# A hybrid attention block on one core: the scheduler's machine model is exchanged

## The chip, the cores and the metric

The kernel runs on one NeuronCore of a Trainium2 chip. The metric is the device time of one execution in microseconds (us). The core has a matrix engine (PE, TensorE), three engines for elementwise work (DVE, the vector engine; ACT, the scalar engine; POOL, GpSimd) and SP (SyncE), which here only issues DMAs. Each engine works through its own list of instructions in order. Between engines, semaphores hold an instruction back until what it reads is written and what it overwrites has been read.

## What is computed

One layer of a streaming encoder on 512 rows of width 1024, all in float32. Three sub-layers, each with an RMS norm before and after it, are added to the residual:

```python
h = rms_norm(x, g_mix_pre)
q_f, k_f, v_f, f_logit, q_c, k_c, v_c = jnp.split(h @ w_in, splits, axis=-1)
o_f = fox_attention(q_f, k_f, v_f, log_sigmoid(f_logit + b_fgate))   # 8 heads of 64, causal
o_c = chunked_rel_attention(q_c, k_c, v_c, rel_bias)                 # 8 heads of 64, banded
mix = jnp.concatenate([rms_norm(o_f, g_fox_out), rms_norm(o_c, g_chunk_out)], -1) @ w_out
x = x + rms_norm(mix, g_mix_post)
ca = memory_cross_attention(rms_norm(x, g_mem_pre), rms_norm(mem, g_mem_kv), w_mem_q, w_mem_kv, w_mem_o)
x = x + rms_norm(ca, g_mem_post)                                     # 4 heads of 256, 256 memory rows
x = x + rms_norm(swiglu(rms_norm(x, g_ffn_pre), w_gate_up, w_down), g_ffn_post)
```

## The kernel before

Every large float32 product is made of three matmuls: each operand is split into a high part `hi` and a rest `lo`, and `mm3` (lines 142 to 146) adds hi·hi, lo·hi and hi·lo into one PSUM bank. Weights come by DMA into three `raw` buffers (line 121); ACT makes `hi` by a cast (line 125) and DVE `lo` by a subtraction (line 126), into two buffers each. A *unit* is one such piece of weights, numbered in the order of use.

The work in the order of the program, with the time it takes place in the profiled execution before:

- 0 to 52 us: x is loaded and normalised, V of the first groups, q and k of the first group.
- 59 to 239 us: sixteen attention heads. `head` (line 524) takes four blocks of 128 rows. For each block PE makes the scores (lines 533 and 534), DVE adds the bias and takes the maximum (line 537), ACT makes the exponential and its sum (line 547), DVE the reciprocal (line 548) and the product with it (line 549), PE the transposes (line 552), ACT the high part of the transposed probabilities, `pth` (line 554), DVE the rest, `ptl` (line 555). After four blocks PE multiplies with V (line 561), ACT and DVE combine the two halves (lines 569 and 570). `pair_out` (line 572) does the split of each pair's output (lines 573 and 574). The probabilities `p` have three buffers.
- Between the heads stand dense matmuls that don't depend on them: q, k and V of later groups (`group_proj`, line 404, and `proj_blocks`, line 383, whose bank is emptied on DVE at line 391 and split on ACT and DVE at lines 423, 424, 439, 440 and 443) and the half of the output projection that needs only the first eight heads (lines 649 to 659, banks `ps_a387` to `ps_a394`). Heads 9 to 16 take their bias by a DMA (`chunk_bias`, line 516) into one of four buffers.
- `mem_norm` (line 591) normalises the memory (line 596) and splits it into `mT` (lines 599 and 600), at the end of the heads.
- 239 to 283 us: keys and values of the memory, from `mT` (the first bank is `ps_a402`), and the rest of the output projection. 295 to 400: cross-attention, with transposes at line 809. 400 to 465: its output projection and the start of the feed-forward part, with transposes at line 170.
- 465 to 644 us: a stage whose order on PE, DVE and ACT is written out by hand (line 1227). 645 to 760: the down projection, then the end.

PSUM has eight banks, in four kinds: three `a` (dense products), two `s` (scores), two `t` (transposes), one `o` (the products with V).

Outside the written-out stage the order on each engine isn't that of the code. A scheduler of the language plays the program through with a model of the machine: at each step it takes, for an engine that the model has free, the instruction that is ready in the model's time, and among several the one of least priority number. The number is the place in the code, shifted by `later(n)` (line 96). Those that matter here are `later(-20)` for the projections of a group (line 609), `urge[n]` of −205, 150, 0 and −120 for the heads of the four groups (line 602), +100 more for the products with V (line 556), 135 for `mem_norm` (line 636) and −5 for the half of the output projection (line 649). What the model says an instruction takes, and what it waits for, therefore decides what is put in front of what, while on the chip the order is then fixed.

## Time and profile before

| | |
|---|---|
| median of 2 runs | 769.27 us (769.16 to 769.38) |
| the profiled execution, its own time | 769.24 us |
| its span in the trace | 767.5 us |
| PE busy | 752.7 us, 98% of the span |
| DVE busy | 595.7 us, 78% |
| ACT busy | 442.9 us, 58% |
| POOL busy | 63.6 us, 8% |
| TensorE clock granted, mean | 0.997 |
| DMA | 80.05 MB, 104 GB/s |

How to read it: busy time counts the time in which an engine had at least one instruction under way. Matmuls are pipelined, so that neighbours overlap and the busy time of one of them is longer than the distance to the next. In the rows, `L533 MATMUL ps_s<-T,Q` is an instruction of line 533 that writes the tile `ps_s` and reads `T` and `Q`; a number behind a name in the order rows below is the buffer or the tile's serial number.

### The profile page before, as it was taken

How to read it: one execution, taken by the hardware profiler on the slowest of the kernel's cores; microseconds unless marked ns; L12 is line 12 of the kernel's file. 1: busy time of each engine (PE TensorE's matmuls, PEld its weight loads, DVE VectorE, ACT ScalarE, POOL GpSimd, SP SyncE). 2: the span in 40 equal slices, each digit the busy share in tenths (PEclk: the TensorE clock that was granted, in tenths of full speed). 3: DMA queues.
4: the chain of work that ended last, by engine and by line, in shares of the span. 5: the costliest groups of instructions: out<-in, count | busy, mean ns of one | idle time of the engine just before them, and what ended most of it. 6: DMA issues, size and time to landing. Idle time of an engine off the chain costs nothing.

```text
span 767.5 us, 12862 instructions
## 1 busy us (share of the span) xinstructions
PE 752.7 (98%) x4988; PEld 674.4 (88%) x4988; DVE 595.7 (78%) x1083; ACT 442.9 (58%) x811; POOL 63.6 (8%) x105
## 2 busy tenths in 40 slices
PE   9999999999999999999999999999999999999996
PEld 9977888887778988877778899999999999898985
DVE  8667889789886688555653897999999999987746
ACT  7558889667875457444563635555555557543411
POOL 1001132100321201000001200000000000000001
PEclk9999999999999999999999999999999999999998
DMA  7522123422323735421341132333333323233312
GB/s 268 145 64 76 29 56 95 126 83 60 109 80 83 265 120 186 118 76 59 108 147 48 56 102 65 110 111 110 111 111 110 111 84 110 83 115 107 108 58 109
DMA packets 60748, 80.05 MB, mean 104 GB/s; under 512 B 2704, under 2 KB 43664, under 8 KB 60688
## 3 DMA queue, kind: packets, MB, share of 16 engines
q1 hardware_dynamic: 59264, 74.49, 30.9%
q0 software_dynamic: 1280, 4.72, 1.8%
q8 instruction: 39, 0.64, 0.4%
q14 instruction: 21, 0.17, 0.1%
q10 hardware_dynamic: 144, 0.02, 0.0%
HBM read 77.13 MB, written 2.10 MB: 103 GB/s over the span
## 4 chain that ended last, share of the span: by engine, by line
PE 87%; ACT 6%; DVE 4%; issue 2%; POOL 1%; DMA 1%; DVEq 0%; POOLq 0%; ACTq 0%
PE ps_a L144 13%; PE ps_a L146 13%; PE ps_a L143 13%; PE ps_t L1130 3%; PE ps_t L1127 3%; PE ps_s L1128 3%; PE ps_t L1128 3%; PE ps_s L1127 3%; PE ps_s L1130 3%; PE ps_s L143 2%; PE ps_s L146 2%; PE ps_s L144 2%; PE ps_t L552 2%; PE ps_o L561 2%; PE ps_s L533 1%
## 5 line engine op out<-in xcount | busy, mean ns | idle before, releaser
L126 DVE TENSOR_TENSOR lo<-raw,hi 128x1024 fp32r<-128x1024 f32 x56 | 68.2, 1223 | 20.6 <-ACT hi L125 20.4
L146 PE MATMUL ps_a<-hTh,lo 128*128 128x512 f32 x192 | 76.7, 399 | 0.0
L144 PE MATMUL ps_a<-hTl,hi 128*128 128x512 f32 x192 | 75.9, 395 | 0.0
L143 PE MATMUL ps_a<-hTh,hi 128*128 128x512 f32 x192 | 75.9, 395 | 0.0
L125 ACT CAST hi<-raw 128x1024 fp32r<-128x1024 f32 x56 | 57.8, 1047 | 25.5 <-PE ps_a L144 21.2
L923 DVE TENSOR_TENSOR ring_lo<-sums,ring_hi 128x1024 fp32r<-128x1024 f32 (+1 forms) x39 | 46.7, 1196 | 12.9 <-ACT ring_hi L922 8.5
L922 ACT CAST ring_hi<-sums 128x1024 fp32r<-128x1024 f32 (+1 forms) x39 | 40.1, 1029 | 17.2 <-PE ps_s L1128 15.6
L922 ACT CAST ring_hi<-fraw 128x1024 fp32r<-128x1024 f32 (+1 forms) x26 | 26.7, 1033 | 33.5 <-DVE fraw L1009 13.9
L923 DVE TENSOR_TENSOR ring_lo<-fraw,ring_hi 128x1024 fp32r<-128x1024 f32 (+1 forms) x26 | 31.0, 1201 | 14.2 <-ACT ring_hi L922 14.0
L144 PEld LDWEIGHTS ps_a<-hTl,hi 128*128 128x128 f32 x192 | 36.1, 188 | 6.4
L146 PEld LDWEIGHTS ps_a<-hTh,lo 128*128 128x128 f32 x192 | 36.1, 188 | 6.4
L143 PEld LDWEIGHTS ps_a<-hTh,hi 128*128 128x128 f32 x192 | 36.2, 188 | 5.6
L547 ACT ACTIVATE p<-p,nm 128x128 f32<-128x128 f32 (+1 forms) x64 | 36.1, 565 | 8.1 <-DVE nm L537 7.2
L554 ACT CAST pth<-ps_t 128x128 fp32r<-128x128 f32 (+1 forms) x64 | 27.0, 424 | 14.5 <-PE ps_t L552 13.7
L555 DVE TENSOR_TENSOR ptl<-ps_t,pth 128x128 fp32r<-128x128 f32 (+1 forms) x64 | 30.7, 487 | 5.0 <-ACT pth L554 3.7
L552 PE MATMUL ps_t<-ident,p 128*128 128x128 f32 x160 | 28.2, 275 | 1.1 <-DVE p L549 0.8
L549 DVE TENSOR_SCALAR p<-p,rc 128x128 f32<-128x128 f32 (+1 forms) x64 | 26.8, 418 | 0.1
L552 PEld LDWEIGHTS ps_t<-ident,p 128*128 128x128 f32 x160 | 19.3, 140 | 7.3 <-issue 2.4
L143 PE MATMUL ps_a<-hi,oh 128*128 128x512 f32 x64 | 25.5, 399 | 0.0
L1130 PE MATMUL ps_a<-b,ring_lo 128*128 128x256 f32 (+1 forms) x93 | 25.5, 276 | 0.0
L1127 PE MATMUL ps_a<-b,ring_hi 128*128 128x256 f32 x92 | 25.5, 277 | 0.0
L1128 PE MATMUL ps_a<-b,ring_hi 128*128 128x256 f32 x92 | 25.4, 276 | 0.0
(546 smaller groups left out, 2760.9 us busy)
## 6 DMA issues: line engine op xcount, KB each, us to landing
raw<-in_dram SPq DMA_DIRECT2D x64, 512.0 KB, 3.9
fraw<-in_dram SPq DMA_DIRECT2D x26, 512.0 KB, 3.5
place<-in_dram SPq DMA_DIRECT2D x21, 512.0 KB, 4.3
more_room<-in_dram SPq DMA_DIRECT2D x15, 512.0 KB, 4.3
cb<-in_dram SPq DMA_DIRECT2D x8, 256.0 KB, 2.7
xo<-in_dram POOLq DMA_DIRECT2D x4, 512.0 KB, 7.6
out_dram<-yd SPq DMA_DIRECT2D x8, 256.0 KB, 2.0
rawv<-in_dram SPq DMA_DIRECT2D x3, 520.0 KB, 6.3
```

Of the source, the lines that this page charges most:

```text
L125: act.copy(hi[:, j : j + n, :], raw)
L126: dve.tensor_tensor(out=lo[:, j : j + n, :], in0=raw, in1=f32(hi[:, j : j + n, :]), op=ALU.subtract)
L143: pe.matmul(dst, sh, mh, start=first, stop=False)
L144: pe.matmul(dst, sh, ml, start=False, stop=False)
L146: pe.matmul(dst[:, to], sl, mh[:, to], start=False, stop=last)
L547: act.activation(p[:, :n], p[:, :n], AF.Exp, bias=nm, scale=-1.0, accum_out=sm)
L552: pe.transpose(tp[:, k * P : (k + 1) * P], p[:, k * P : (k + 1) * P], ident)
L922: act.copy(h2, v)
L923: dve.tensor_tensor(out=l2, in0=v, in1=f32(h2), op=ALU.subtract)
L1127: pe.matmul(dst, w[0][:, k, :], b[:, 0, k, :], start=first and k == 0, stop=False, skip_group_check=more)
L1128: pe.matmul(dst, w[0][:, k, :], b[:, 1, k, :], start=False, stop=False, skip_group_check=more)
L1130: pe.matmul(dst[:, to], w[1][:, k, :], b[:, 0, k, to], start=False, stop=last and k == 3, skip_group_check=more,)
```

## The change

It hands the context that schedules the program one more argument. The instructions are the same 7012 in both programs; only the order on the engines differs.

```diff
@@ -1517,7 +1517,7 @@
     args.append(nc.dram_tensor("out_0_dram", (SEQ, D), _mybir.dt.float32, kind="ExternalOutput").ap())
-    with _tile.TileContext(nc) as tc:
+    with _tile.TileContext(nc, schedule_with_timeline_sim=True) as tc:
         hybrid_block_kernel(tc, *args)
```

The order is the same from 465 us of before through the written-out stage and in the last 60 us. It differs on PE, DVE and ACT in the attention heads, in the cross-attention, in the start of the feed-forward part and in the first 55 us of the down projection. Three places show it; the first is on PE, at the score matmul of head 11, block 2 (`ps_s262_2078`; `ps_a296` and `ps_a297` are projections of the last group, `ps_a394` is the last bank of the half output projection). Before:

```order
L552 MATMUL ps_t245_2004<-ident_69,p10_2_1996 128x128 x3
L146 MATMUL ps_a296_2337<-hTh_82,lo8_2212 128x512
L143 MATMUL ps_a297_2369<-hTh_82,hi8_2211 128x512
L144 MATMUL ps_a297_2369<-hTl_83,hi8_2211 128x512
L533 MATMUL ps_s262_2078<-T101_1859,Q101_1783 128x384
L534 MATMUL ps_s262_2078<-L2_420,Q101_1783 128x384
L552 MATMUL ps_t250_2021<-ident_69,p10_3_2013 128x128 x4
L146 MATMUL ps_a297_2369<-hTh_82,lo8_2212 128x512
L143 MATMUL ps_a297_2369<-hTh_82,hi8_2211 128x512
```

After:

```order
L144 MATMUL ps_a394_2964<-lo11_2847,oh_623 128x512
L146 MATMUL ps_a394_2964<-hi11_2846,ol_624 128x512
L552 MATMUL ps_t245_2004<-ident_69,p10_2_1996 128x128 x3
L533 MATMUL ps_s262_2078<-T101_1859,Q101_1783 128x384
L534 MATMUL ps_s262_2078<-L2_420,Q101_1783 128x384
L552 MATMUL ps_t250_2021<-ident_69,p10_3_2013 128x128 x4
L533 MATMUL ps_s267_2095<-T101_1859,Q101_1783 128x512
L534 MATMUL ps_s267_2095<-L2_420,Q101_1783 128x512
L561 MATMUL ps_o251_2028<-pth1_410,V10_1597 128x512
L552 MATMUL ps_t256_2058<-ident_69,p11_0_2050 128x128
L561 MATMUL ps_o251_2028<-ptl1_411,V10_1597 128x512
```

All 166 dense matmuls from `ps_a297` to `ps_a394` that stood behind this score matmul now stand ahead of it, and behind it no dense matmul follows until `ps_a402`.

The second place is on DVE, in the heads 12 and 13 (`p12`, `p13`: probabilities of these heads; `qk`: a projection on its way out of PSUM; `lo10`: the rest of weight unit 10). Before:

```order
L548 RECIPROCAL rc286_2165<-sm285_2164 128x1
L555 TENSOR_TENSOR ptl1_411<-ps_t282_2154,pth1_410 128x2x128
L549 TENSOR_SCALAR p12_2_2162<-p12_2_2162,rc286_2165 128x384
L537 ISA p12_3_2179,nm289_2180<-ps_s288_2176,cb3_2125 128x512
L537 ISA nm289_2180 128x1
L570 TENSOR_TENSOR o11_2043<-ps_o272_2113,ot11_2122 64x512
L391 TENSOR_TENSOR qk_2394<-ps_a297_2369,rrow_67 128x512
L126 TENSOR_TENSOR lo10_2402<-raw10_0_2403,hi10_2401 128x1024
L555 TENSOR_TENSOR ptl1_411<-ps_t287_2170,pth1_410 128x3x128
L548 RECIPROCAL rc291_2182<-sm290_2181 128x1
L424 SCALAR_TENSOR_TENSOR Q111_2396<-qk_2394,Q111_2396 64x512
L549 TENSOR_SCALAR p12_3_2179<-p12_3_2179,rc291_2182 128x512
```

After:

```order
L537 ISA p12_3_2179,nm289_2180<-ps_s288_2176,cb3_2125 128x512
L537 ISA nm289_2180 128x1
L549 TENSOR_SCALAR p12_2_2162<-p12_2_2162,rc286_2165 128x384
L548 RECIPROCAL rc291_2182<-sm290_2181 128x1
L537 ISA p13_0_2497,nm301_2498<-ps_s300_2494,cb4_2491 128x128
L537 ISA nm301_2498 128x1
L549 TENSOR_SCALAR p12_3_2179<-p12_3_2179,rc291_2182 128x512
L570 TENSOR_TENSOR o11_2043<-ps_o272_2113,ot11_2122 64x512
L555 TENSOR_TENSOR ptl1_411<-ps_t282_2154,pth1_410 128x2x128
L555 TENSOR_TENSOR ptl1_411<-ps_t287_2170,pth1_410 128x3x128
L548 RECIPROCAL rc303_2500<-sm302_2499 128x1
L537 ISA p13_1_2512,nm306_2513<-ps_s305_2509,cb4_2491 128x256
```

The rows of the projections and weights (lines 126, 391, 424) have left this place for one further ahead; reductions, reciprocals, products and subtractions of neighbouring blocks follow one another.

The third place is on PE, in the cross-attention, at the first transposes of line 809 (`ps_t444`; `ps_a452` and `ps_a466` are projections to the queries of later heads, `ps_s` scores). Before:

```order
L144 MATMUL ps_a452_3809<-hTl2_3420,hi23_3656 128x512
L146 MATMUL ps_a452_3809<-hTh2_2998,lo23_3657 128x512
L143 MATMUL ps_a452_3809<-hTh2_2998,hi23_3656 128x512
L809 MATMUL ps_t444_3742<-ident_69,xp0_3720 128x128 x2
L144 MATMUL ps_a452_3809<-hTl2_3420,hi23_3656 128x512
L809 MATMUL ps_t444_3742<-ident_69,xp0_3720 128x128 x2
L146 MATMUL ps_a452_3809<-hTh2_2998,lo23_3657 128x512
L143 MATMUL ps_a452_3809<-hTh2_2998,hi23_3656 128x512
```

After:

```order
L146 MATMUL ps_a466_3952<-hTh2_2998,lo24_3800 128x512
L143 MATMUL ps_s454_3864<-kT_2997,qq_3421 128x256
L144 MATMUL ps_s454_3864<-kT_2997,qq_3421 128x256
L146 MATMUL ps_s454_3864<-kT_2997,qq_3421 128x256
L143 MATMUL ps_a466_3952<-hTh2_2998,hi24_3799 128x512
L144 MATMUL ps_a466_3952<-hTl2_3420,hi24_3799 128x512
L809 MATMUL ps_t444_3742<-ident_69,xp0_3720 128x128 x4
L146 MATMUL ps_a466_3952<-hTh2_2998,lo24_3800 128x512
L143 MATMUL ps_a466_3952<-hTh2_2998,hi24_3799 128x512
```

17 dense matmuls of the next block (`ps_a466`) and more of `ps_a453` stand between the scores and their transposes, and the four transposes stand together.

On SP the bias loads of heads 9 to 16 stand some places later among the loads of weights, among them those of heads 9 to 12 ahead of one weight load of the output projection; POOL's order is nearly unchanged.

## The prediction

> **What bounds the kernel now.** I read the page's head and its slices first, then the share of the chain by engine, then the waits of PE, then windows of the stretch that the change rearranges.
>
> ```profile
> PE 752.7 (98%) x4988; PEld 674.4 (88%) x4988; DVE 595.7 (78%) x1083; ACT 442.9 (58%) x811; POOL 63.6 (8%) x105
> ...
> PE   9999999999999999999999999999999999999996
> ...
> DVE  8667889789886688555653897999999999987746
> ...
> PEclk9999999999999999999999999999999999999998
> ...
> PE 87%; ACT 6%; DVE 4%; issue 2%; POOL 1%; DMA 1%; DVEq 0%; POOLq 0%; ACTq 0%
> ```
>
> PE is busy in 98% of the span and holds 87% of the chain: the kernel is bound by the number of matmuls, and almost nothing can be won. The waits of PE say how little: the longest is 1.1 us, at the start of the program (the first row), and those of the cross-attention and the start of the feed-forward part (lines 809 and 170) are the others here; columns: total us, times, longest.
>
> ```profile
> PE ps_t L241 <- DVE ones L80: 1.1, 1, 1.1
> ...
> PE ps_t L809 <- DVE xp L804: 0.7, 2, 0.5
> PE ps_t L170 <- DVE b L183: 0.4, 1, 0.4
> PE ps_t L170 <- DVE y L161: 0.2, 1, 0.2
> PE ps_t L170 <- DVE f L181: 0.2, 1, 0.2
> ```
>
> The bound is a mean over the span, though. In the attention, up to 239 us, softmax work on DVE and ACT and transposes on PE run in a chain, and dense matmuls of later projections fill the gaps. The windows show how close the second engine is there (columns: stretch, its length, busy time and instructions of PE, PEld, DVE, ACT, POOL, then clock, DMA share, GB/s).
>
> ```profile
> 173.10:239.10 66.00, 63.66 (x331) 50.60 (x329) 57.23 (x151) 51.40 (x109) 12.63 (x12) 1.00 0.24 73
> 62.40:173.10 110.70, 108.77 (x654) 93.40 (x654) 93.66 (x261) 88.41 (x208) 21.03 (x42) 1.00 0.25 72
> 404.47:420.79 16.32, 16.32 (x73) 13.52 (x72) 5.76 (x9) 4.99 (x9) 2.54 (x3) 1.00 0.11 32
> 640.00:660.00 20.00, 20.00 (x120) 17.65 (x119) 20.00 (x39) 12.97 (x21) 0.57 (x1) 1.00 0.38 132
> ```
>
> DVE has 57.23 of 66.0 us of work in the last six heads and 93.66 of 110.7 before them. Take the dense matmuls out of the first stretch and DVE, not PE, sets its length.
>
> **The dense matmuls that move.** The last place where both orders can be laid on one another is the first score matmul of head 11, block 2 (the first order pair above). Everything that stood ahead of it before stands ahead of it after, and 166 matmuls of 512 columns more: 70 of the q and k projections of the last group (buffers 297, 298, 299) and 96 of the half of the output projection that needs only the first eight heads (387 to 394). The rows of that moment before:
>
> ```profile
> 170.59 0.33 PE L533 MATMUL ps_s<-T,Q 128*128 128x384 f32 x1
> ...
> 173.15 0.54 DVE L537 CUSTOM_DVE_ANT_0 p<-ps_s,cb 128x384 f32<-128x384 f32 x1
> ```
>
> One dense matmul costs its slot, not its busy time, since neighbours overlap in the pipeline: the window at 404.47 holds nothing but 72 of them, with 72 weight loads, in 16.32 us, so 0.2267 us each. 166 × 0.2267 = 37.6 us, and the score matmul goes from 170.59 to about 208.2. [...]
>
> These 37.6 us aren't work added. They leave the stretch from the reduction of head 11, block 2, at 173.15, to the split of the memory at line 600, after which PE goes on with the memory's keys in both orders:
>
> ```profile
> 234.01 0.79 DVE mm L596 x2
> 234.82 1.92 ACT mT L599
> 236.76 2.30 DVE mT L600
> 239.11 0.38 PE ps_a L144
> ```
>
> PE's remainder in this stretch is at most 66.0 − 37.6 = 28.4 us. If the stretch could shrink to that, the move would cost nothing. It can't, because of DVE.
>
> **What DVE keeps in the bare stretch.** With the fillers go the DVE instructions that prepare or empty them. Busy time in the stretch, by line, in this order: 126 (split of weights), 391 (empty a projection), 424 and 440 (split q and k):
>
> ```profile
> 173.10:239.10 66.00, 7.55 (x6) 1.00 0.24 73
> ...
> 173.10:239.10 66.00, 2.04 (x3) 1.00 0.24 73
> ...
> 173.10:239.10 66.00, 2.75 (x4) 1.00 0.24 73
> ...
> 173.10:239.10 66.00, 2.73 (x4) 1.00 0.24 73
> ```
>
> Together 15.07 us, now (second order pair) under dense PE work further ahead: there DVE gets 93.66 + 15.07 = 108.7 us for 110.7 + 37.6 = 148.3 us of PE, which hides it. 57.23 − 15.07 = 42.2 us stay. Two subtractions of line 555 (three and four blocks wide) now stand behind line 600 and no longer delay it, −1.1 us by the mean of the group below (487 ns each, wider than the mean). So 41.1.
>
> ```profile
> L547 ACT ACTIVATE p<-p,nm 128x128 f32<-128x128 f32 (+1 forms) x64 | 36.1, 565 | 8.1 <-DVE nm L537 7.2
> ...
> L555 DVE TENSOR_TENSOR ptl<-ps_t,pth 128x128 fp32r<-128x128 f32 (+1 forms) x64 | 30.7, 487 | 5.0 <-ACT pth L554 3.7
> ...
> L549 DVE TENSOR_SCALAR p<-p,rc 128x128 f32<-128x128 f32 (+1 forms) x64 | 26.8, 418 | 0.1
> ```
>
> Is 41.1 us attainable on an engine that waits now and then? Two ends. Packed: neighbours on DVE overlap a little. The 128-column reduction before starts at 169.91, lasts 0.29, and its neighbour starts 0.22 later. If two thirds of the 134 instructions left save 0.07 each, 6.3 us go, and 34.8 are the lower end. Loose: if DVE stays as busy as before, 57.23 of 66.0, the 41.1 become 47.4. Between them lie the round trips from the reduction over the exponential (565 ns and its accumulator's read) to the reciprocal. The new order (second order pair) puts the multiply, subtract or reduction of a neighbouring block in between, so that I estimate 1 us a head over packed work: 34.8 + 5.4 heads × 1 = 40.2. I take 41.1, the busy time itself.
>
> ```profile
> 169.57 0.19 ACT L547 ACTIVATION_READ_ACCUMULATOR p<-p,nm 128x1 f32 x1
> ...
> 169.91 0.29 DVE L537 CUSTOM_DVE_ANT_0 p<-ps_s,cb 128x128 f32<-128x128 f32 x1
> 170.13 0.08 DVE L537 DVE_READ_ACCUMULATOR2_ANT nm<- 128x1 f32 x1
> ```
>
> The net of the move: +37.6 − (66.0 − 41.1) = +12.7 us. ACT can't bind: from its 51.40 us at least the casts of weights, q and k leave as well.
>
> **Weights that come late.** The projections run closer behind one another, and hi and lo have two buffers each, so a weight unit is split into the pair that the matmuls two units earlier have just read. For four units only 1.7 to 3.1 us of PE work (counted in the new order, at the slots of before) stand between the last reader and the first use; one cast and one split take
>
> ```profile
> L126 DVE TENSOR_TENSOR lo<-raw,hi 128x1024 fp32r<-128x1024 f32 x56 | 68.2, 1223 | 20.6 <-ACT hi L125 20.4
> ...
> L125 ACT CAST hi<-raw 128x1024 fp32r<-128x1024 f32 x56 | 57.8, 1047 | 25.5 <-PE ps_a L144 21.2
> ```
>
> 1.05 + 1.22 = 2.27 us. At 2.27 against 1.7 to 3.1, I take 0.25 us each, +1.0; ends 0 and +4 (a cast that finds ACT busy with an exponential, four times).
>
> **Cross-attention and start of the feed-forward part.** There the new order puts more dense matmuls ahead of the transposes that waited (third order pair). If the four waits above vanish, −1.5 us; ends 0 and −3, since each switch between transposes and dense matmuls has its own cost and there are fewer. I take −1.5.
>
> **The down projection.** The windows show DVE full, 20.00 of 20.00 us, at 640 to 660. One split moves behind two others there. The same work in another order under a full DVE: I take 0, ends −1 and +1.5.
>
> **POOL and SP.** The bias loads of the chunk heads stand some places later among SP's weight loads, and one weight load of the output projection stands behind four of them. The bias buffers they wait for are those of heads that end tens of us earlier: 0. POOL's order is nearly the same: 0. In the written-out stage and from 700 us on the order is the old one: 0.
>
> **Sum** against the profiled run, 769.24 us (span 767.5 and 1.7 around it; the median of the runs is 769.27): +12.7 + 1.0 − 1.5 + 0 = +12.2, so 781.4 us, 1.6% more. About 2%, 753.9 and 784.7 us, is what a measurement of this kernel can tell from no change.
>
> **Rivals.**
> First, DVE packs better than I think, and is over before it matters: 34.8 us give +6.4, with −1.5 and no late weights 774.1; fewer switches on PE could bring 771.5. For it: DVE showed 20.00 of 20.00 us busy at 640, so it can pack when fed. Against it: there its work is independent, here each multiply waits for an exponential. Even a stretch of 28.4 us would give only 767.7: faster by 2% can't be had by moving matmuls on an engine that is busy 98%.
> Second, on the slower side, the bare heads pack no better than the filled ones: three buffers of probabilities, two banks for scores and two for transposes hold the blocks in step, and PE's own queue, in order, makes each wait longer. At 47.4 us the move costs +19.0 and the total is 787.7. It decides from 44.3 us in the stretch (line 600 ending after 256) upward; late weights at their +4 end have the same effect from 41.3.
> Third, the clock. PE would be busy for 28.4 of 41 us. The trace of before shows what a nearly idle PE gets (0.27 of 7 us busy, clock 0.70), and what it keeps with gaps under 1.1 us (1.00):
>
> ```profile
> 760.00:767.00 7.00, 0.27 (x3) 0.07 (x1) 3.08 (x8) 1.02 (x4) 0.54 (x1) 0.70 0.39 150
> ```
>
> If the clock halved through the stretch, its 28.4 us would become up to 56.8, 15.7 more than DVE's 41.1, and the total 797. The gaps that I find between PE's instructions in the new order are about 1 us, so that it should keep 1.00. [...]
>
> **Chances.** The forecast (775 to 785) 0.52; the first rival (below 775) 0.18; the second (785 to 792) 0.25; the clock 0.03; faster by over 2% 0.02. The range of 8 in 10 runs from the first rival's 771.5 to 789, beyond the second's 787.7. Faster 0.02, within 2% 0.70, slower 0.28.
>
> **What would show it.** Right: the score matmul of head 11, block 2, starts near 209 (208 to 213); from the following reduction to the end of line 600 it takes 39 to 44 us, with DVE over 90% busy and PE 65 to 75%, clock 1.00; line 600 ends near 253; the lead of before stays about the same from there to the end, and shrinks by 1 to 2 us between 290 and 465. Wrong: heads after 209 with DVE under 88% busy (second rival), a clock below 0.95 there (third), or stalls over 1 us on line 143 at weight units before 209.

## The result: 812.7 us, 5.6% slower, and the profile after

The changed kernel takes 812.7 us (median of 2 runs, 811.81 and 813.60) against 769.27 before: ratio 1.056, 95% interval 1.0543 to 1.0577. The prediction was 781.4, its range ended at 789.0. The profiled execution took 813.60 us, its span is 811.6, 44.1 us longer than before.

From the page of the kernel after, the rows that answer those of before: busy time by engine, the busy slices of PE and DVE and the granted clock, and the chain by engine.

```profile
PE 771.5 (95%) x4988; PEld 690.1 (85%) x4988; DVE 596.6 (74%) x1083; ACT 444.5 (55%) x811; POOL 61.0 (8%) x105
...
PE   9999999989977799989998999999999999999996
...
DVE  8666679664788568735564379999999899988745
...
PEclk9999999999989799999999999999999999999999
...
PE 83%; DVE 7%; ACT 6%; issue 3%; DMA 0%; POOL 0%; DVEq 0%; POOLq 0%; ACTq 0%
```

The reader is to see three things. PE, at 90% or more in every slice but the last before, falls to between 70 and 80% in the twelfth to fourteenth slice (223 to 284 us). DVE is less busy than before in seven of the eight slices ahead of them. And the clock, 1.00 before up to the tail, drops there too (0.86 from 224.74 to 272.56 us). The waits of PE, whose longest was 1.1 us, now begin with these (total us, times, longest):

```profile
PE ps_s L533 <- DVE nm L537: 6.6, 11, 1.4
PE ps_t L552 <- DVE ptl L555: 4.2, 4, 2.0
PE ps_o L561 <- ACT pth L554: 2.5, 2, 1.8
PE ps_t L552 <- DVE rc L548: 2.2, 2, 1.9
PE ps_a L143 <- ACT hTh L179: 2.0, 1, 2.0
PE ps_a L143 <- ACT oT L825: 2.0, 3, 0.9
PE ps_a L143 <- DVE V L351: 1.6, 1, 1.6
```

The timeline of the kernel after gives the three moments on which the sum of the prediction rested:

```profile
219.54 0.44 PE L533 MATMUL ps_s<-T,Q 128*128 128x384 f32 x1
...
224.74 0.53 DVE L537 CUSTOM_DVE_ANT_0 p<-ps_s,cb 128x384 f32<-128x384 f32 x1
...
270.27 2.29 DVE L600 TENSOR_TENSOR mT<-mm,mT 128x2048 fp32r<-128x2048 f32 x1 [1.18 <-ACT mT L599]
```

Beside the starts of the same instructions before, and later ones taken from the timelines in the same way:

| moment | before | after | later by | forecast |
|---|---|---|---|---|
| score matmul of head 11, block 2 | 170.59 | 219.54 | 49.0 | 38.6 |
| its reduction on DVE | 173.15 | 224.74 | 51.6 | 38.6 |
| end of line 600 | 239.06 | 272.56 | 33.5 | 13.7 |
| rest of the output projection (`ps_a406`) | 261.69 | 298.90 | 37.2 | 13.7 |
| last bank of the projection after the cross-attention, first half (`ps_a497`) | 399.03 | 443.28 | 44.3 | 12.2 |
| written-out stage (`ps_t538`) | 465.17 | 508.75 | 43.6 | 12.2 |
| end of the span | 767.5 | 811.6 | 44.1 | 12.2 |

So every part of the attention cost more than forecast: the front by 10.4 us, the step to the reduction by 2.6, the bare stretch by 6.8, the memory's keys by 3.7. The cross-attention turned from −1.5 to about +7.

### The profile page after: what moved, and what is told of

The parts are those of the page before. It is cut to its first block, busy times and chain, and to the rows that moved or that the text cites. A ratio compares the mean times of both kernels' runs of the same rounds, so it can differ in the third digit from the quotient of the medians.

```text
span 811.6 us, 12892 instructions
## 1 busy us (share of the span) xinstructions
PE 771.5 (95%) x4988; PEld 690.1 (85%) x4988; DVE 596.6 (74%) x1083; ACT 444.5 (55%) x811; POOL 61.0 (8%) x105
## 4 chain that ended last, share of the span: by engine, by line
PE 83%; DVE 7%; ACT 6%; issue 3%; DMA 0%; POOL 0%; DVEq 0%; POOLq 0%; ACTq 0%
PE ps_a L143 14%; PE ps_a L144 14%; PE ps_a L146 14%; PE ps_t L1130 3%; PE ps_t L1127 3%; PE ps_s L1130 3%; PE ps_s L1127 3%; PE ps_t L1128 3%; PE ps_s L1128 3%; PE ps_s L143 2%; PE ps_s L144 2%; PE ps_s L146 2%; PE ps_o L561 1%; PE ps_a L1130 1%; PE ps_a L1128 1%
## 5 line engine op out<-in xcount | busy, mean ns | idle before, releaser
L146 PEld LDWEIGHTS ps_a<-hTh,lo 128*128 128x128 f32 x192 | 36.9, 192 | 9.7 <-DVE lo L126 2.5
L144 PEld LDWEIGHTS ps_a<-hTl,hi 128*128 128x128 f32 x192 | 36.9, 192 | 7.9 <-DVE hTl L183 0.9
L533 PE MATMUL ps_s<-T,Q 128*128 128x256 f32 (+1 forms) x64 | 24.0, 378 | 7.3 <-DVE nm L537 6.6
L1127 PE MATMUL ps_a<-b,ring_hi 128*128 128x256 f32 x92 | 25.5, 277 | 0.0
L144 PE MATMUL ps_a<-lo,oh 128*128 128x512 f32 x64 | 25.3, 395 | 0.2 <-DVE lo L126 0.2
```

Source lines behind the costliest of these rows:

```text
L144: pe.matmul(dst, sh, ml, start=False, stop=False)
L146: pe.matmul(dst[:, to], sl, mh[:, to], start=False, stop=last)
L1127: pe.matmul(dst, w[0][:, k, :], b[:, 0, k, :], start=first and k == 0, stop=False, skip_group_check=more)
```

## The experiments

Most of these kernels hold an order given from outside. They have the instructions of the kernel and this addition, which ties each instruction of an engine behind the one named ahead of it, for the issue only; `ORDER` is a table of names by engine.

```diff
         hybrid_block_kernel(tc, *args)
+        _in_order(tc, nc, _mybir, _lists(ORDER))
+
+def _in_order(tc, nc, mybir, lists):
+    at = {i.name: i for i in nc.cur_bb.bb.instructions}
+    issue_only = mybir.DependencyInfo(mybir.DependencyClass.NoSync, mybir.DependencyReason.DATA)
+    for row in lists:
+        for one, two in zip(row, row[1:]):
+            tc.add_manual_dep(at[two], one, issue_only, reason="order")
```

### Where the loss is made: two halves put together

The first kernel takes the lists of before up to the instructions that start by 239 us, and those of after behind them; the second the other way round.

> All engines keep the order of before up to the start of the memory's keys (239 us of before), and the order of after from there on. Theory: the loss has two parts of their own, about 37 us made in the attention and about 7 us made in the cross-attention and behind it by the order there; this run keeps only the second, so 774 to 780 us. Rival: the later part loses only because the attention hands it late weights and a cold clock; then 768 to 771 us.

> The order of after up to the start of the memory's keys, and the order of before from there on. Theory: 803 to 808 us, the attention's part alone, line 600 ending about 33 us later than before. Rival: 810 to 814 us, as after, since the later loss would follow from the attention.

Measured: 776.02 us (ratio 1.0083, 1.0054 to 1.0113) and 806.19 us (1.0475, 1.0437 to 1.0514). Both lie in the theory's span. 6.75 and 36.9 us add up to 43.7, and the whole loss is 43.4: the attention and the part behind it lose independently. The sum holds to some 2 us only, by which single runs of these kernels differ (805.19 and 807.20 for the second).

### The cross-attention: one place

> The order of before on all engines up to 320 us of before (the normalisation ahead of the cross-attention and its transposes included), the order of after from there on. Theory: of the 6.75 us that the later part cost alone, most (2.2 + 0.7 us of waits and about 1.7 us of half clock) come from one place, where two splits of a weight unit stand on ACT and DVE ahead of the normalised rows that PE waits for, and that place is now as before: 770.5 to 773 us. Rival: the loss sits in the output projection of the cross-attention (waits of 0.5 to 1.1 us six times): 774 to 777 us.

Measured: 771.78 us (1.0034, 1.0023 to 1.0045). About 4 of the 6.75 us are made between 239 and 320 us of before. The timeline of the kernel after shows where: ACT does two casts of weights (line 125) and DVE two splits (line 126) ahead of the short rows of lines 179 and 183, and PE stands for 2.05 us.

```profile
345.12 1.99 ACT L125 CAST hi<-raw 128x1024 fp32r<-128x1024 f32 x2
347.01 0.84 ACT L179 ACTIVATE hTh<-ps_t,gn 128x256 fp32r<-128x256 f32 x2
...
346.20 2.36 DVE L126 TENSOR_TENSOR lo<-raw,hi 128x1024 fp32r<-128x1024 f32 x2 [0.25 <-ACT hi L125]
...
347.54 0.97 PE L143 MATMUL ps_a<-hTh,hi 128*128 128x512 f32 x3 [2.05 <-ACT hTh L179]
```

The next kernel changes only this place of the kernel after; on ACT (on DVE lines 126 and 183 in the same way):

```diff
-L125 CAST hi_3656<-raw_0_3658 128x1024
-L125 CAST hi_3656<-raw_4_3662 128x1024
 L179 ACTIVATE hTh_2998<-ps_t_3570,gn 128x256
 L179 ACTIVATE hTh_2998<-ps_t_3579,gn 128x256
+L125 CAST hi_3656<-raw_0_3658 128x1024
 L179 ACTIVATE hTh_2998<-ps_t_3570,gn 128x256
 L179 ACTIVATE hTh_2998<-ps_t_3579,gn 128x256
+L125 CAST hi_3656<-raw_4_3662 128x1024
```

> The kernel after with one place changed, at 345 us: on ACT two, on DVE two of the rows that make the normalised input of the cross-attention's queries stand ahead of the casts and splits of weight unit 23 instead of behind them. Theory (PE waits 2.2 + 0.7 + 0.3 us for rows that stand behind 2.4 us of splits, and the low use that follows halves the clock for 3.4 us): the waits shrink to about 1 us, no half clock near 349, 808.5 to 810 us. Rival (the third dense matmul there needs unit 23 itself, so that the wait only moves to it): 811.5 to 813.5 us.

Measured: 809.82 us (807.29 to 810.71; 1.0516, 1.05 to 1.0532), 2.9 us below the median of after. The waits of PE between 330 and 360 us are now

```profile
PE ps_a L143 <- ACT hi L125: 0.6, 1, 0.6
PE ps_a L143 <- ACT hTh L179: 0.2, 1, 0.2
```

against 2.0 + 0.5 in after, and the half clock at 349 us is gone. In the profiled executions 0.7 us of the difference are there by `ps_a406` (298.16 instead of 298.90), ahead of the changed place, and 4.1 at the first transposes of line 809 (375.80 instead of 379.88): the order of the rows at this place costs about 3 us.

### The clock: more work, less time

The windows of the kernel after, cut in steps of 3.41 us from the edges of its half-clock stretches (the shortest ahead of the tail last 3.41 us; columns as in the prediction), in pairs: a window in which PE does little, and the next one.

```profile
168.20:171.61 3.41, 1.50 (x10) 0.84 (x8) 3.32 (x8) 2.22 (x7) 0.29 (x2) 1.00 0.32 90
171.61:175.03 3.42, 3.24 (x8) 2.57 (x9) 2.43 (x6) 2.74 (x5) 0.14 (x1) 0.50 0.02 5
181.85:185.27 3.42, 1.72 (x10) 1.29 (x11) 3.36 (x6) 1.89 (x4) 0.00 (x0) 1.00 0.58 169
185.27:188.68 3.41, 3.41 (x18) 3.41 (x18) 0.01 (x1) 0.00 (x0) 2.31 (x2) 0.50 0.43 138
...
345.69:349.11 3.42, 1.07 (x4) 0.59 (x4) 3.17 (x5) 2.29 (x5) 0.00 (x0) 1.00 0.21 70
349.11:352.52 3.41, 3.41 (x8) 2.64 (x9) 1.11 (x3) 0.74 (x2) 0.00 (x0) 0.50 0.90 258
```

In each pair the clock is 0.50 in the window that follows the one of low use (1.50, 1.72 and 1.07 us of PE work), though PE is busy for 3.24 to 3.41 us of it. In the second and third pair it is full of dense matmuls, which take nearly twice their time: those of 256 columns start 0.21 us apart instead of 0.11, those of 512 columns 0.43 instead of 0.23.

What the first two pairs cost is told by the second kernel of the two halves (the attention of after). Up to the memory's keys its order is that of after on every engine, and the waits of PE at these places are as long (1.2 us for line 555, 1.6 for line 351), but in its profile no window of the front is halved. From 165 to 195 us, after and then this kernel:

```profile
165.00:195.00 30.00, 25.87 (x134) 21.50 (x133) 16.10 (x29) 13.92 (x25) 4.03 (x6) 0.89 0.23 73
```

```profile
165.00:195.00 30.00, 25.85 (x147) 21.34 (x146) 18.22 (x38) 15.56 (x29) 5.64 (x8) 1.00 0.29 96
```

In the same 30 us it does 13 matmuls more. From 164 to 193 us it gains 3.1 us on after, half of it in each of the two windows, and its score matmul of head 11, block 2, starts at 217.01 instead of 219.54. Two more kernels leave the front of after as it is, the one with the place at 345 us and the one with less DVE work (below). Their profiles have one of the two half windows, and the score matmul starts at 218.76 and 218.62.

From 222.8 to 277.4 us the clock of after is halved for 20.5 us in all (6.83 + 3.41 + 10.24). To see what this costs, PE gets work that nobody needs (shown in part; a second table names the instructions ahead of which it stands):

```diff
+        tc.extra = extra = []
         with later(-115):
             for c in range(4):
                 hi, lo = unit()
                 acc = bank("a")
+                if c == 0:
+                    for _ in range(55):
+                        extra.append(pe.matmul(acc, oh[:, 0, :P], oh[:, 0, :], start=True, stop=True))
```

> The kernel after in its own order on every engine, with 55 matmuls of 512 columns more on PE (12.5 us at 0.2267 us each), whose products nobody reads (they go to the bank of the memory's first keys before it is begun). They stand ahead of 16 instructions for which PE waits in the last heads, each group shorter than that wait. Theory (PE is so little used there that the granted clock halves, and the half clock costs time): the clock stays at 1.00 from 219 to 280 us, and the kernel is 2 to 6 us faster than after, 807 to 811 us, in spite of 12.5 us more work on PE. Rival (the half clock costs nothing, since PE waits there anyway): same as after or slower, 812 to 820 us.

Measured: 810.32 us (808.72 to 813.59; 1.0535, 1.0506 to 1.0565), 2.4 us below after, though single runs overlap with it. The windows of this kernel, for the bare stretch and for 260 to 280, and below them those of after:

```profile
224.74:272.56 47.82, 40.66 (x209) 28.80 (x210) 40.79 (x131) 32.12 (x82) 11.96 (x12) 1.00 0.16 49
260.00:280.00 20.00, 16.29 (x106) 13.56 (x107) 12.53 (x32) 8.86 (x17) 2.58 (x4) 1.00 0.01 1
```

```profile
224.74:272.56 47.82, 34.12 (x162) 25.30 (x161) 40.67 (x132) 32.31 (x82) 11.90 (x12) 0.86 0.16 50
...
260.00:280.00 20.00, 15.36 (x70) 13.25 (x71) 11.64 (x31) 7.18 (x15) 1.95 (x2) 0.66 0.00 1
```

The clock stays at 1.00, as the theory had it, and the gain is where dense work meets the full clock: `ps_a406` starts at 296.49 instead of 298.90. Line 600 starts at 270.10 instead of 270.27: in the bare heads themselves the full clock, with the added work to pay for, gains next to nothing, as the rival had it. How much each of the two does alone isn't shown.

### The bare stretch: load or round trips

In heads 12 to 16 the subtraction of line 555 works on one column, so the rest of the probabilities is left out there; the order is that of after.

```diff
-                dve.tensor_tensor(out=span(pl, i), in0=t3, in1=f32(span(ph, i)), op=ALU.subtract)
+                part = (slice(None),) * 3 if nhead[0] < 12 else (slice(None), slice(0, 1), slice(0, 1))
+                dve.tensor_tensor(out=span(pl, i)[part], in0=t3[part], in1=f32(span(ph, i))[part], op=ALU.subtract)
```

> The kernel after in its own order; in heads 12 to 16 the subtraction of line 555 (now 556) works on one column instead of the whole block, so that the rest of the probabilities is left out there: about 8.3 us less DVE time (20 times 0.42), the same number of rows and waits, PE and ACT unchanged. Theory (DVE's load with its waits sets the length of the bare stretch): the stretch from the reduction of head 11, block 2, to line 600 falls from 47.8 to 39 to 43 us, the kernel to 804 to 808 us. Rival (the round trips between PE, DVE and ACT set it and DVE's load fits into them): the stretch falls by less than 2.5 us, 810 to 813 us.

Measured: 810.59 us (1.0531, 1.0512 to 1.055), in the rival's span. From the reduction to the end of line 600:

```profile
223.82:269.76 45.94, 32.51 (x161) 24.22 (x161) 36.47 (x134) 32.26 (x82) 11.74 (x12) 0.85 0.17 52
```

DVE does 4.2 us less than in the stretch of after (40.67 to 36.47), half of the 8.3 that were meant to go (the shortened rows still take 0.15 us each). The stretch is 1.9 us shorter, so a little under half of the load that went is won. That is too small a dose to part theory and rival cleanly, but it isn't DVE's load alone that fills 47.8 us: with 79% busy DVE the heads still need 45.9. In the profiled execution 0.9 us of the kernel's lead over after are there ahead of the stretch, at the score matmul.

### The front

> The kernel after with one place changed in the front, at 168 us: on DVE the subtractions of line 555 for head 8, blocks 0 and 1, stand ahead of one split of q (line 424) and the sum of line 570 instead of behind them, on ACT their casts (line 554) ahead of the copy of line 569. Theory (PE waits 1.4 us for the bank that these rows free, and the low use halves the clock from 171.6 to 175.0 us, which costs 1.6 us): that half clock goes, head 9 and all behind it come 2 to 3 us earlier, 809.5 to 811 us. Rival (the heads are late anyway, the gain is lost at the next wait): 812 to 814 us.

On DVE, the edit is this (ACT's line 554 moves ahead of 569 in the same way):

```diff
+L555 TENSOR_TENSOR ptl_411<-ps_t_1526,pth_410 128x128
+L555 TENSOR_TENSOR ptl_411<-ps_t_1541,pth_410 128x2x128
 L424 SCALAR_TENSOR_TENSOR Q_2364<-qk,Q_2364 64x512
 L570 TENSOR_TENSOR o_1392<-ps_o_1481,ot_1490 64x512
-L555 TENSOR_TENSOR ptl_411<-ps_t_1526,pth_410 128x128
-L555 TENSOR_TENSOR ptl_411<-ps_t_1541,pth_410 128x2x128
```

Measured: 812.09 us (811.32 to 815.56; 1.0541, 1.0523 to 1.0559), no gain. Some waits of PE from 160 to 220 us, of the kernel after and then of this one:

```profile
PE ps_a L143 <- DVE V L351: 1.6, 1, 1.6
PE ps_t L552 <- DVE ptl L555: 1.2, 1, 1.2
...
PE ps_s L533 <- DVE nm L537: 0.6, 1, 0.6
...
PE ps_a L143 <- DVE qk L391: 0.3, 1, 0.3
```

```profile
PE ps_a L143 <- DVE qk L391: 1.7, 1, 1.7
PE ps_a L143 <- DVE V L351: 1.6, 1, 1.6
...
PE ps_t L552 <- DVE ptl L555: 0.2, 1, 0.2
```

The wait for the bank fell from 1.2 to 0.2 us, and the one for line 391 grew from 0.3 to 1.7. A half clock still follows, at 172.8 us. The half clock that the theory counts on isn't a fixed cost of this place: in the profiles of three kernels with the unchanged order it doesn't come (see the clock, above).

### Spreading the dense matmuls again

```diff
+                    with tc.issue_after(starts[(10, 10, 11, 12, 13, 13, 14, 15)[4 * half + t]].ins):
                         for k in range(4):
```

The diff is shown in part: the lines that fill `starts` with the first score matmul of each head are missing. The loop is that of the half output projection. The new model orders the rest.

> The kernel after, with the 96 matmuls of the half output projection issued behind the first score matmul of heads 11 to 16, one or two banks each. Theory: the front gets 21.8 us shorter, the stretch of the last heads hides them in PE's idle time and grows by less than 6 us, and the clock stays at 1.00 there: 788 to 797 us. Rival: DVE sets the stretch so closely that the matmuls and their waits lengthen it by most of 21.8 us: above 803 us.

Measured: 813.79 us (1.0574, 1.054 to 1.0609): the rival's number, but neither mechanism came out as stated. The front became 10.5 us shorter (209.06 for the score matmul of head 11, block 2), not 21.8: PE waits there for the heads, and the stretch grew by 8.8 us, between the theory's 6 and the rival's "most of 21.8" (line 600 starts 59.5 us behind that matmul, in after 50.7). The largest waits of PE from 168 to 209 us (the lines stand three or so lower than in after: 534 is 533, 540 is 537); the first was 0.6 us in the rows of after above:

```profile
PE ps_s L534 <- DVE nm L540: 4.5, 3, 3.3
PE ps_a L143 <- DVE V L351: 2.8, 1, 2.8
```

Here the dense matmuls stand among the heads in blocks of twelve; the order of before puts them there a few at a time (the first order pair shows three in a row, then two). That the size of the blocks holds the heads up is likely, but no run changed it alone.

### One engine's list with another model's rest

> Only the order on PE is that of after; DVE, ACT, POOL and SP are ordered by the old model around it. Theory (the dense matmuls drawn ahead on PE make the loss, the other engines' order little): 800 to 812 us. Rival (the order on DVE and ACT, where weight splits stand ahead of short operations that PE waits for, makes 10 us in the front and 7 in the cross-attention): 788 to 797 us.

> The kernel after, with PE alone held to its order of before; DVE, ACT, POOL and SP are ordered by the new model around it. Theory (the order on PE decides, and the new model serves a given PE order well): 768 to 775 us. Rival (the new model's order on DVE and ACT is bad by itself, and holding one engine while another model orders the rest costs as it did with the PE order of after): 790 us or more.

Measured: 843.97 us (1.0966, 1.0934 to 1.0999) and 804.65 us (1.0456, 1.0431 to 1.0481). The first misses both spans, on the slow side. The second hits the rival, with PE's list of the fast kernel. So no engine's list carries the time alone: the same PE list gives 769 or 805 us, and the other one 813 or 844, with the lists beside it. Why a model orders the rest so badly around a list that isn't its own was not tried further.

### A try to beat both

> The kernel before in its own order, but in 32 places of ACT and DVE a cast or split of weights stands one to three rows later, behind a short row that PE needs sooner and that was ready. Theory (splits ahead of short rows cost PE some tenths of a us each): 766.5 to 768.8 us, faster than before by up to 0.4%. Rival (PE's waits in before lie elsewhere): 769 to 770 us.

Measured: 773.96 us (1.0054, 1.004 to 1.0068): slower by 4 us, outside both spans. The time is lost in small steps, 2.4 us by the start of `ps_a406` and 4.7 by `ps_a497`; which of the 32 places cost it was not tried. The move that gains 3 us at 345 us of the kernel after isn't a rule.

### The pieces together

> The kernel after with the changed place at 168 us, the changed place at 345 us and the 55 extra matmuls of the last heads together. Theory (three separate losses, each a wait or low use and the half clock behind it): the gains add, 803.5 to 806.5 us, and what stays over before, about 35 us, is the bunched dense matmuls and the round trips of the bare heads. Rival (they overlap): 807 to 810 us.

Measured: 807.20 us (806.28 to 808.49; 1.0485, 1.0469 to 1.05). That is the rival's number, since the theory counted on a gain in the front. The gains of the place at 345 us and of the extra matmuls add (2.9 + 2.4 = 5.3; measured 5.5); the place in the front gives nothing here either. About 37 us over before stay.

## Why the prediction was wrong

Of the 44.1 us, 12.2 were forecast. The signs that the prediction gave for being wrong came: DVE was under 88% busy in the bare heads (85%), the clock there under 0.95 (0.86), and PE stood for 1.6 us on line 143 before the score matmul, though for V and not for a weight.

**What bounds the kernel, and that almost nothing can be won:** not contradicted; none of the kernels here is faster than before.

**The front, the largest miss.** The 166 dense matmuls that move are right in number, and their 37.6 us is a part of what was measured. The front came 49.0 us later, 11.4 more. The term for this, "weights that come late", was put at +1.0 with an end of +4. It failed, mis-sized and partly misnamed. The waits of PE up to that score sum up to 8.4 us (from 60 to 219.5 us), against 2.0 before (57 to 170.6). The longer ones, of after and then of before:

```profile
PE ps_a L143 <- DVE V L351: 1.6, 1, 1.6
PE ps_s L533 <- DVE nm L537: 1.4, 2, 0.9
PE ps_a L146 <- DVE lo L126: 1.2, 3, 0.5
PE ps_t L552 <- DVE ptl L555: 1.2, 1, 1.2
PE ps_a L143 <- ACT hi L125: 0.8, 1, 0.8
PE ps_a L144 <- DVE lo L126: 0.8, 2, 0.6
```

```profile
PE ps_s L533 <- ACT fb L503: 1.0, 2, 0.7
PE ps_a L143 <- DVE V L351: 0.5, 1, 0.5
```

Weights (lines 125 and 126) make 2.8 of the 8.4; the rest is V, banks of scores and of transposes, and smaller ones. The half clock, for which the front had no term, makes another 3.1. The 6.4 us of added waits and these 3.1 are 9.5 of the 11.4 us. Most of the loss lies between the first scores of head 9 and of head 10: 37.3 us, of which the slots of PE's matmuls, priced by the distances in before, fill 26 to 28, and 13.7 before, of which they fill 12 to 13. The one try to take a single wait out moved it to the next.

**What DVE keeps in the bare stretch.** The load was right to 0.5 us (41.1 forecast, 40.67 in the window above). The step that failed is "I take 41.1, the busy time itself". The stretch took 47.8, a little beyond the loose end of 47.4: DVE is 85% busy there, with the dense matmuls in between it was 87%. The estimate of 1 us a head of round trips stood for about 2.4 (47.8 − 34.8, over 5.4 heads). With less DVE load the stretch stayed at 45.9, so the load alone isn't what fills it. The waits of PE from 219 to 273 us sum up to 15.7 us; the largest are for two kinds of banks that DVE has yet to empty, scores (line 533 behind 537, 5.2) and transposes (552 behind 555, 3.0). Whether the banks decide or the round trips themselves stays open: another division of the eight banks wasn't tried. The second rival had the price of this term and named these banks, at 0.25; its total of 787.7 had none of the loss in the front.

**The clock:** the third rival, at 0.03, was wrongly put down. That gaps of "about 1 us" would "keep 1.00" failed: waits were up to 2.05 us, and the clock halved six times before the end. The half clock costs 3.1 us in the front, about 2.2 from line 600 to `ps_a406` (28.63 us in after, 26.39 with the extra matmuls), where the forecast missed 3.7 in all, and up to 1.7 (half of 3.41) at 349 us. In the bare stretch it costs next to nothing, where the rival had put 15.7.

**Cross-attention and feed-forward start:** −1.5 forecast, about +7 measured up to `ps_a497`, then −0.7. I counted the waits that would vanish, and not what the order puts ahead of the short rows on ACT and DVE: there I read PE's list alone. One such place costs about 3 us. That a switch between dense matmuls and transposes has a cost shows in the trace of before: from 330.32 to 331.31 us two dense matmuls and four transposes of line 809 take 0.99 us, while their slots (0.227 and 0.109 us each) sum up to 0.89.

**Down projection, POOL, SP, the written-out stage:** 0 forecast; 43.6 at the start of the written-out stage became 44.1 at the end, and through that stage nothing changed. In the down projection more rows change places than the one split that I named, on PE too. No wait of PE in after is for POOL or a DMA.

The attention's 37 us are shown to be made there (two halves, adding up). 2.4 us of the clock and about 3 of the place at 345 us are shown by taking them away, 3.1 more of the clock by two profiles of one order. That the rest is the bunching of dense work with round trips behind it rests on the windows and waits; no kernel here undid the bunching finely enough to take it away but the order of before itself.

## What to carry to other kernels

A list of instructions that keeps PE busy early was no gain here, where a second engine works at 87% beside it: dense matmuls are the filling of a chain's waits, and spent ahead of it they leave the waits bare. Price a bare chain by the busy share that its second engine reached with the filling (47.4 us for the 47.8 measured), not by its busy time (41.1). When an order moves, read every engine's list at the places where PE waits, not PE's list alone.

## What the runs showed of the hardware

In the kernel after the granted clock fell behind stretches of low use of PE. In its trace the clock changes only at moments that lie whole multiples of 3.4133 us apart, to 2 ns, and is 1.00 or 0.50 between them; ahead of the last 14 us the half stretches are 3.41, 3.41, 6.83, 3.41, 10.24 and 3.41 us long. With the span up to there cut in these steps, the four full-clock windows in which PE was busy least (0.77, 1.07, 1.50 and 1.72 us, from 263.77, 345.69, 168.20 and 181.85) were each followed by a half one. Of the six with 2.00 to 2.32 us two were (2.09 from 219.40, 2.32 from 256.95), and none with more, so the busy time alone doesn't part them. Half windows with 2.44, 2.15 and 2.68 us (from 222.81, 267.19 and 270.60) were followed by another half one, those with 3.24 us or more by a full one. In the kernel before the least busy window ahead of the tail had 2.23 us (from 237.12), and the clock stayed at 1.00; in its tail a window with 0.91 us (from 759.36) was followed by 0.50. The longest wait of PE in the kernel after was 2.05 us, ahead of the half window at 349.11.

The same order in the front had two half windows in two profiles (after, and with the extra matmuls), one in two others (with the place at 345 us, and with less DVE work) and none in a fifth (the attention of after), worth 3.1 us between two and none. I put this down to where the steps of the clock lie in the program; no run moved them alone. Such kernels also scattered more, as far as a few runs tell: the five runs with one place changed in the front went from 811.32 to 815.56 us, the seven of before beside them from 769.26 to 770.7.
